# A hybrid decoder layer on one core: output weight sums made among the pairs, keys four tiles at a time, row sums of squares on ScalarE, and new orders at stage ends

## The chip, the core and the metric

The kernel runs on one core of one Trainium2 chip. The metric is the device time of one execution in microseconds (us); the median of three runs is compared. A core has a matrix engine, TensorE (PE, with its weight loads shown apart as PEld), a vector engine, VectorE (DVE), an activation engine, ScalarE (ACT), GpSimd (POOL), and SyncE (SP). Here SP issues most transfers from memory; POOL issues stores and accumulating loads.

## What is computed

One layer over 1024 tokens of width 1024, with 256 memory tokens, in float32:

```python
h = rms_norm(x, norm_g); z = h @ w_in                      # 11 blocks of 1024 columns
u = gelu(z_u); v = layer_norm(gelu(z_v))                   # branch A: chunked spatial gate
br_a = u * (tril(w_s) @ v + b_s) * silu(z_ga)              # in chunks of 128 tokens
glu = z_ba * sigmoid(z_bb)                                 # branch B
br_b = silu(layer_norm(causal_depthwise_conv(glu, 31 taps))) * silu(z_gb)
k, v = split(rms_norm(mem) @ w_kv)                         # branch C: 4 heads of 256
br_c = softmax(q k^T / 16) v * silu(z_gc)
merged = sum over n of sigmoid(z_mn) * (br_n @ w_branch[n])
out = rms_norm(x + merged @ w_out, final_norm_g)
```

## The kernel before

All products are made of float32 operands split in two halves, a rounded high half (ACT, `split`, line 74) and the rest as low half (DVE, line 75); three matmuls (high by high, high by low, low by high) stand for one. A matmul takes 128 x 128 weights and 256 or 512 columns. Engines run their instructions in order, each with its own queue. The order on a queue is not the one written: a planner lays out the instructions at build time by modelled costs, earlier written ones first among those that are ready, and hands out buffers as they come free. Loads marked `keep` stay in their written order on SP. Buffers: 39 slots of 1024 columns (`slot`), 6 for operands (`op`), 3 for raw weights, 4 each of `sum` and `half`.

Stages, in order of time:

- **Keys** (line 231). For each of 8 key tiles `e`, 8 steps of the contraction times 3 matmuls of 256 columns; the weights of one tile come as one transfer of 512 KB, and all of the memory (transposed, with its gain, `mhi` and `mlo`) is needed by the first tile. `mean_rsqrt` sums squares over partitions with one-column f32 matmuls (line 109); `spread` brings a row of factors to all partitions with f32 matmuls on diagonal matrices (lines 120, 121). `sumsq` makes squares on ACT and adds them on DVE.
- **Values** (line 280), 96 matmuls of 512 columns; then branch A's `v` by token (line 322), during which the sums of squares of x are finished, spread and used.
- **Pairs** (lines 364 to 414): 4 rounds of 10 blocks; each pair makes two column tiles of a block by a Strassen scheme with 7 products of 12 matmuls, accumulated in the banks x, y and z. `pend` carries the last two products into the next pair. `pump(n)` lets n steps of the depthwise convolution run on DVE between pairs; `spump` does the same for `wsum`, which loads quarters of branch B's output weights, adds them by accumulating loads on POOL, splits the sum and stores both halves for the later product.
- **Branch projections** A and C (line 656, `merge`), with attention in between. In C's, the convolution's channel mean and variance are made (`center`, `conv_rstd`) and `normed` finishes branch B's tiles `cm`.
- **Branch B's projection** and then **the output projection** (line 864, `oprod`): 7 products each, again by Strassen's scheme, on 2 x 2 blocks of 512. A product is 4 blocks of 12 matmuls, one for each 128 rows, accumulated in `px` or `py`; two blocks share one tile of two banks. Branch B's weight sums come from memory (`swload`); the output weights are loaded raw (`wraw`), subtracted (`sub`, line 957), and split (`wsplit`) on the spot.
- **End** (`yadd`): the residual is added, rows are squared and summed on ACT, scaled and stored.

Of the kernel before, what the change touches and what calls it, by code (L numbers as in the profile page):

```python
# [16 lines left out]
P = 128  # L17
# [22 lines left out]
def trunk(ctx, tc, xt, x, memt, wf, wv, wkf, wkv, wbr, wb1, wo, wst, bs, cols, fng, out):  # L40
# [66 lines left out]
    def mean_rsqrt(ssum, n, eps, ps):  # L107
        for i in range(n):
            T.matmul(ps[:, i:i + 1], ssum[:, i * P:(i + 1) * P], ones[:, 0:1], start=True, stop=True)
        a = small.tile([P, n], F32, tag=f"ms{n}", name=nm("ms"))  # L110
        V.tensor_scalar(a, ps[:, :n], 1.0 / D, eps, ALU.mult, ALU.add)
        return rsqrt(a, n)

    def spread(r, n, dst, mk):
        for i0 in range(0, n, 4):
            w = min(4, n - i0)
            ps = mk()
            for i in range(w):
                dg = small.tile([P, P], F32, tag="dg", name=nm("dg"), bufs=4)
                V.tensor_scalar(dg, ident, r[:, i0 + i:i0 + i + 1], None, ALU.mult)  # L120
                T.matmul(ps[:, i * P:(i + 1) * P], ones, dg, start=True, stop=True)
            A.copy(dst[:, i0 * P:(i0 + w) * P], ps[:, :w * P])

# [22 lines left out]
    onesd = const.tile([P, P], F32, name="onesd")  # L146
    G.memset(onesd, 1.0 / D)
# [9 lines left out]
    ahead = []  # L157

    def kv_ahead(n):
        i = len(ahead)  # L160
        while i < min(n, 2 * KT):
            t = slot(s="kvraw")
            keep(nc.sync.dma_start(out=t, in_=wkf[i] if i < KT else wkv[i - KT]))
            ahead.append(t)
            i += 1

    ahead.append(slot(s="kvraw"))
    mraw = [slot(shape=(P, 4, M), s="mraw") for _ in range(2)]
    keep(nc.sync.dma_start(out=ahead[0][:, :H], in_=wkf[0][:, :H]))
    keep(nc.sync.dma_start(out=mraw[0][:, :2, :], in_=memt[0][:, :2, :]))  # L170
    keep(nc.sync.dma_start(out=mraw[0][:, 2:, :], in_=memt[0][:, 2:, :]))
    keep(nc.sync.dma_start(out=ahead[0][:, H:], in_=wkf[0][:, H:]))
    keep(nc.sync.dma_start(out=mraw[1], in_=memt[1]))
    kv_ahead(2)
    xr = [None] * KT

    def x_load(k):
        xr[k] = slot(s="xr")
        keep(nc.sync.dma_start(out=xr[k], in_=xt[k]))

    mhi2 = [slot(F32R, (P, 4, M), "mhi") for _ in range(2)]
# [3 lines left out]
    for k in range(KT):  # L185
# [5 lines left out]
    xsum = slot(s="xsum")  # L191
    kv_ahead(3)
# [25 lines left out]
    for e in range(KT):  # L218
        kv_ahead(e + NAHEAD)
        x_load(e)  # L220
        if e:
            hi, lo = wchunk(None, ahead[e])
        else:
            hi, lo = op((P, 1024), "whi"), op((P, 1024), "wlo")
            for v in (slice(0, H), slice(H, 2 * H)):
                split(ahead[0][:, v], hi[:, v], lo[:, v])
        ps = bank()
        for k in range(KT):
            ks = slice(k * P, (k + 1) * P)
            for j, (w, m) in enumerate(((hi, mhi), (hi, mlo), (lo, mhi))):  # L230
                T.matmul(ps[:, :M], w[:, ks], m[k], start=(k == 0 and j == 0), stop=(k == KT - 1 and j == 2))  # L231
        late.append((e, ps))
        if e == 0:
            msum = slot(s="msum")[:, :M]
            for k in range(KT):
                sumsq(mraw[k // 4][:, k % 4, :], msum, k == 0, M)
        if e == E0:
            mr = mean_rsqrt(msum, MT, RMS_EPS, bank())
        if e == E1:
            spread(mr, MT, mrb, bank)  # L240
        if e >= E1:
            while late:
                k_out(*late.pop(0))
        if e >= XLAG:
            x_gain(e - XLAG)

# [11 lines left out]
    nsq = 0  # L258

    def squares(n):  # L260
        nonlocal nsq
        for k in range(nsq, min(nsq + n, KT)):
            sumsq(xr[k], xsum, k == 0, S)
            nsq = k + 1

    for hf in range(2):
        pst = [bank() for _ in range(MT)]
        for c in range(4):
            kv_ahead(KT + hf * 4 + c + NAHEAD)
            hi, lo = wchunk(None, ahead[KT + hf * 4 + c])  # L270
            i = hf * 4 + c
            if i < XLAG:
                x_gain(KT - XLAG + i)
# [8 lines left out]
            if i >= SQ0:  # L282
                squares(1)
# [25 lines left out]
    for th in range(2):  # L309
        va = [slot(s="va") for _ in range(4)]  # L310
        for ch in range(2):
            pst = [bank() for _ in range(4)]
            for c in range(4):
# [11 lines left out]
                if th == 0:  # L325
                    if i == 0:
                        squares(KT)
                        xrs = mean_rsqrt(xsum, TT, RMS_EPS, bank())
                        rb = slot(s="rb")
                        spread(xrs, TT, rb, bank)  # L330
                    else:
# [41 lines left out]
    def pair(blk, p, consume):  # L373
# [12 lines left out]
        o12 = operand(a12)  # L386
        V.tensor_tensor(s3, a11, a21, ALU.subtract)
        V.tensor_tensor(s4, a12, s2, ALU.subtract)
        prod(z, o12, B[1][0], True, True)
        ca, cb = slot(s="ca"), slot(s="cb")  # L390
# [718 lines left out]
```

## Time and profile before

| | |
|---|---|
| median of 3 runs | 1335.52 us (1333.23 to 1335.55) |
| profiled execution | 1335.1 us |
| its span, first to last instruction | 1333.2 us |
| PE busy | 1308.3 us (98%) |
| DVE busy | 1107.5 us (83%) |
| ACT busy | 612.8 us (46%) |
| mean granted clock of PE | 0.996 |
| moved by DMA | 219.84 MB, 165 GB/s over the span |

Rows of the profile name an instruction by its line in the kernel, engine, operation and the tiles that it writes and reads (out<-in). Matmuls are pipelined, and their ends are modelled, so a matmul's duration is longer than the distance to the next.

### The profile page before, as it was taken

The numbers are of one execution on the slowest core, as the hardware profiler recorded it, in microseconds if no ns is written. First come the engines' busy times: TensorE is split into PE (matmuls) and PEld (weight loads), VectorE is DVE, ScalarE is ACT, GpSimd is POOL, SyncE is SP. The second block draws the span as 40 slices with busy tenths as digits, with TensorE's granted clock in tenths as the row PEclk, the third lists the DMA queues.
The fourth block names the chain that finished last, engine by engine and source line by source line (L and its number), as shares of the span: only waits on it lengthen the run. The fifth ranks groups of instructions, "written<-read, shape, count | busy, mean of one in ns | idle before, by whom it ended". The sixth has DMA issues, their size and how long they took to land.

```text
span 1333.2 us, 16301 instructions
## 1 busy us (share of the span) xinstructions
PE 1308.3 (98%) x6036; PEld 1090.6 (82%) x6036; DVE 1107.5 (83%) x1506; ACT 612.8 (46%) x1005; POOL 88.8 (7%) x162
## 2 busy tenths in 40 slices
PE   8999999999999999999999999999999999999896
PEld 7888888888888888888888888887888888888785
DVE  6799769979977997986996996796797486975996
ACT  6757645434444444534444444345543352442345
POOL 0000000111100110100100000001000010000000
PEclk9999999999999999999999999999999999999999
DMA  9634444554634554454543214338554354657513
GB/s 375 245 109 160 141 144 146 170 166 145 195 128 141 172 174 153 173 135 157 154 150 125 95 48 127 123 114 302 180 182 174 114 218 157 240 213 283 211 32 127
DMA packets 72223, 219.84 MB, mean 165 GB/s; under 512 B 7248, under 2 KB 16592, under 8 KB 72144
## 3 DMA queue, kind: packets, MB, share of 16 engines
q1 hardware_dynamic: 50512, 140.79, 30.8%
q0 software_dynamic: 21344, 77.60, 17.3%
q8 instruction: 47, 0.77, 0.2%
q10 hardware_dynamic: 288, 0.42, 0.1%
q14 instruction: 32, 0.26, 0.1%
HBM read 156.92 MB, written 61.87 MB: 164 GB/s over the span
## 4 chain that ended last, share of the span: by engine, by line
PE 91%; DVE 5%; ACT 2%; issue 1%; DMA 0%; SPq 0%; DVEq 0%; ACTq 0%
PE x L365 33%; PE y L365 16%; PE acc L656 13%; PE z L365 8%; PE acc L864 7%; PE b L322 6%; PE b L231 2%; PE acc L694 2%; PE acc L730 2%; PE b L280 1%; PE sp L534 1%; DVE y L972 1%; DVE op L75 1%; DVE gate L957 1%; DMA mraw<-in_memt 0%
## 5 line engine op out<-in xcount | busy, mean ns | idle before, releaser
L365 PE MATMUL x<-T,op 128*128 128x512 f32 x1440 | 347.5, 390 | 0.7 <-ACT u L404 0.7
L365 PEld LDWEIGHTS x<-T,op 128*128 128x128 f32 x1440 | 269.9, 188 | 57.4 <-ACT u L404 1.1
L74 ACT CAST op<-sum 128x512 fp32r<-128x512 f32 x160 | 99.4, 622 | 131.2 <-PE z L365 50.7
L456 DVE SCALAR_TENSOR_TENSOR conv<-cb,col,conv 128x994 f32<-128x994 f32 (+14 forms) x120 | 151.9, 1266 | 0.5
L75 DVE TENSOR_TENSOR op<-sum,op 128x512 fp32r<-128x512 f32 x160 | 109.1, 686 | 25.6 <-ACT op L74 25.2
L365 PE MATMUL x<-B,op 128*128 128x512 f32 x480 | 115.5, 389 | 0.0
L365 PE MATMUL z<-B,op 128*128 128x512 f32 x480 | 115.3, 389 | 0.0
L365 PE MATMUL y<-T,op 128*128 128x512 f32 x480 | 115.3, 389 | 0.0
L365 PE MATMUL y<-B,op 128*128 128x512 f32 x480 | 115.3, 389 | 0.0
L456 DVE SCALAR_TENSOR_TENSOR conv<-ca,col,conv 128x994 f32<-128x994 f32 (+14 forms) x90 | 113.9, 1266 | 0.3
L74 ACT CAST op<-raw 128x512 fp32r<-128x512 f32 x120 | 74.3, 620 | 78.9 <-PE y L365 77.4
L75 DVE TENSOR_TENSOR op<-raw,op 128x512 fp32r<-128x512 f32 x120 | 82.0, 687 | 29.7 <-ACT op L74 29.5
L365 PEld LDWEIGHTS y<-B,op 128*128 128x128 f32 x480 | 90.1, 188 | 18.7
L365 PEld LDWEIGHTS y<-T,op 128*128 128x128 f32 x480 | 90.1, 188 | 18.7
L365 PEld LDWEIGHTS x<-B,op 128*128 128x128 f32 x480 | 90.1, 188 | 18.7
L365 PEld LDWEIGHTS z<-B,op 128*128 128x128 f32 x480 | 90.1, 188 | 18.7
L656 PE MATMUL acc<-bhi,whi 128*128 128x512 f32 x256 | 80.3, 395 | 0.9 <-DVE ca L414 0.9
L656 PE MATMUL acc<-bhi,wlo 128*128 128x512 f32 x256 | 79.7, 390 | 0.0
L656 PE MATMUL acc<-blo,whi 128*128 128x512 f32 x256 | 79.4, 391 | 0.0
L864 PE MATMUL acc<-q,sw 128*128 128x512 f32 x288 | 65.4, 389 | 0.0
L864 PEld LDWEIGHTS acc<-q,sw 128*128 128x128 f32 x288 | 54.1, 188 | 11.2
L404 ACT COPY u<-x 128x512 f32<-128x512 f32 x40 | 23.5, 588 | 80.6 <-PE x L365 80.6
(258 smaller groups left out, 2190.9 us busy)
## 6 DMA issues: line engine op xcount, KB each, us to landing
raw<-in_wf SPq DMA_DIRECT2D x80, 512.0 KB, 3.6
sw<-sw SPq DMA_DIRECT2D x28, 512.0 KB, 6.5
raw<-in_wv SPq DMA_DIRECT2D x16, 512.0 KB, 3.6
raw<-in_wbr SPq DMA_DIRECT2D x16, 512.0 KB, 5.9
gate<-g SPq DMA_DIRECT2D x16, 512.0 KB, 4.9
ws<-in_wb SPq DMA_DIRECT2D x14, 512.0 KB, 4.4
sw<-wsh POOLq DMA_DIRECT2D x14, 512.0 KB, 2.9
sw<-ws POOLq DMA_DIRECT2D x14, 512.0 KB, 3.2
```

What stands on the lines that cost most here:

```text
L74: A.copy(hi, src)
L75: V.tensor_tensor(lo, src, f(hi), ALU.subtract)
L231: T.matmul(ps[:, :M], w[:, ks], m[k], start=(k == 0 and j == 0), stop=(k == KT - 1 and j == 2))
L280: T.matmul(pst[m], a[k][:, ms], w[:, ws], start=(k == 0 and j == 0), stop=(k == KT - 1 and j == 2))
L322: T.matmul(pst[t], q[:, a, ts_], w[:, ws], start=(k == 0 and j == 0), stop=(k == KT - 1 and j == 2))
L365: T.matmul(ps, w[:, a, ks], m[k][:, b, :], start=(start and k == 0 and j == 0), stop=(stop and k == 3 and j == 2), skip_group_check=not start)
L404: A.copy(u3, x)
L456: V.scalar_tensor_tensor(out=a[:, PAD - j:], in0=g[:, :n], scalar=col[:, cw + j:cw + j + 1], in1=a[:, PAD - j:], op0=ALU.mult, op1=ALU.add)
L656: T.matmul(ps[:, hf, :], w[:, ks], m[k][:, hf * H:(hf + 1) * H], start=(k == 0 and j == 0), stop=(k == KT - 1 and j == 2))
L694: T.matmul(ps[:, i, :], q[a][:, d, i * P:(i + 1) * P], kk[:, b, d, :], start=(d == 0 and j == 0), stop=(d == 1 and j == 2))
L730: T.matmul(ps[:, d, :], vv[:, a, m, d * P:(d + 1) * P], p2[b][:, m, :], start=(m == 0 and j == 0), stop=(m == MT - 1 and j == 2))
L864: T.matmul(ps[t], a[k][i][:, ts_], w[k][n], start=(start and k == 0 and j == 0), stop=(k == 3 and j == 2), skip_group_check=not start)
```

## The change

- Keys: the packed key weights are cut so that one transfer holds two steps of the contraction for four tiles. Two groups of four tiles run 4 steps each, each step with 2/8 of the contraction for four accumulators. Ten f32 matmuls on a tile of ones are put first on PE.
- Sums of squares: the memory and x are loaded a second time by rows (tokens on partitions), and ACT's Square accumulates each row's sum. `spread` splits the factors in two halves and uses one 512-column matmul of each half for four diagonals.
- Convolution statistics: sum and sum of squares are split (`wchunk`) and averaged by `tokmean`, which leaves the result in all partitions; `conv_rstd` computes the root there, on 128 x 1024.
- Output weight sums: `wsum` handles the output weights too, so 28 sums instead of 14 are made among the pairs; stores of a sum are issued behind the first load of the next; `spump` makes three steps a pair instead of two. The output projection loads both halves.
- Orders: in the last pair the product into z comes after the copy of x; three tiles of branch A are split before that pair; the pump before it is shorter. The last block of the last product is computed in two halves of 256 columns. Row statistics of the output are accumulated half by half, and the final scaling is shared by DVE (640 columns) and ACT.

```diff
-    def spread(r, n, dst, mk):
+    def diagonals(r, n):
+        rh = small.tile([P, n], F32R, tag=f"rh{n}", name=nm("rh"))
+        rl = small.tile([P, n], F32R, tag=f"rl{n}", name=nm("rl"))
+        split(r, rh, rl)
+        groups = []
         for i0 in range(0, n, 4):
             w = min(4, n - i0)
+            dg = wpool.tile([P, 2, 4, P], F32R, tag="op", name=nm("dg"), bufs=NOP)
+            for j, v in enumerate((rh, rl)):
+                V.tensor_tensor(dg[:, j, :w, :], ident[:, None, :].broadcast_to([P, w, P]),
+                                f(v)[:, i0:i0 + w, None].broadcast_to([P, w, P]), ALU.mult)
+            groups.append((i0, w, dg))
+        return groups
+
+    def spread(groups, dst, mk):
+        for i0, w, dg in groups:
             ps = mk()
...
+            for j in range(2):
+                T.matmul(ps[:, :w * P], onesr, dg[:, j, :w, :].rearrange("p a b -> p (a b)"), start=(j == 0),
+                         stop=(j == 1))
             A.copy(dst[:, i0 * P:(i0 + w) * P], ps[:, :w * P])
+
+    def square(src, dst):
+        A.activation(out=src, in_=src, func=AF.Square, accum_out=dst)
...
+    kload(0, slice(0, H))
+    mload(0)
+    kload(0, slice(H, 2 * H))
+    for j in range(1, 4):
+        mload(j)
+        kload(j)
+    mtok = [slot(s="mtok") for _ in range(MT)]
+    kload(4)
+    for t in range(MT):
+        sload(mtok[t], mem[t * P:(t + 1) * P, :])
+    warm = bank("warm")
+    for _ in range(NWARM):
+        T.matmul(warm[:, :P], ones, ones, start=True, stop=True)
...
+            for kk2 in range(2):
+                k = 2 * j + kk2
+                for e in range(4):
+                    ks = slice(kk2 * H + e * P, kk2 * H + (e + 1) * P)
+                    for n, (w, m) in enumerate(((hi, mhi), (hi, mlo), (lo, mhi))):
+                        T.matmul(pst[e][:, :M], w[:, ks], m[k], start=(k == 0 and n == 0),
+                                 stop=(k == KT - 1 and n == 2))
...
+        if g == 0:
+            k3 = half("k3")
+            A.copy(k3[:, :M], pst[3][:, :M])
+            pst[3] = k3
...
     def squares(n):
+        for _ in range(n):
+            t = min(xtok)
+            square(xtok.pop(t), xss[:, t:t + 1])
+            if t + NRAW < TT:
+                xt_load(t + NRAW)
...
-    def pair(blk, p, consume):
+    def pair(blk, p, consume, last=False):
...
+        def second():
+            o12 = operand(a12)
+            prod(z, o12, B[1][0], True, True)
+            V.tensor_tensor(ca[:, :H], z, p1, ALU.add)
...
+        if not last:
+            second()
...
         u3 = half("u3")
         A.copy(u3, x)
+        if last:
+            second()
...
-    def wsum(i, j):
+    def wsum(w, i, j):
         t = slot(F32R, s="ws")
+        for n, b in enumerate((SUMB, SUMO)[w][i]):
+            src = (wb1, wo)[w][b + j]
             if n:
                 G.dma_start(out=f(t), in_=src, accum_op=ALU.add)
             else:
                 nc.sync.dma_start(out=f(t), in_=src)
+                flush()
             yield
         hi = slot(F32R, s="wsh")
         split(f(t), hi, t)
+        unstored.extend(((sdram[w, i, j][0], f(hi)), (sdram[w, i, j][1], f(t))))
         yield
...
+    csr = wchunk(None, csum)
+
+    def tokmean(v):
+        ps = acc()
+        for hf in range(2):
+            for j in range(2):
+                T.matmul(ps[:, hf, :], onesd, v[j][:, hf * H:(hf + 1) * H], start=(j == 0), stop=(j == 1))
+        return ps
...
     def conv_rstd():
         nonlocal crs
-        crs = mean_rsqrt(csq, TT, LN_EPS, misc())
+        ps = flat(tokmean(wchunk(None, csq)))
+        a, s, y = slot(s="ca"), slot(s="cs"), slot(s="crb")
+        for hf in range(2):
+            v = slice(hf * H, (hf + 1) * H)
+            V.tensor_scalar(a[:, v], ps[:, v], LN_EPS, None, ALU.add)
+            A.activation(out=s[:, v], in_=a[:, v], func=AF.Sqrt)
+            V.reciprocal(out=y[:, v], in_=s[:, v])
+            V.tensor_tensor(s[:, v], y[:, v], y[:, v], ALU.mult)
+            V.tensor_tensor(s[:, v], s[:, v], a[:, v], ALU.mult)
+            V.tensor_scalar(s[:, v], s[:, v], -0.5, 1.5, ALU.mult, ALU.add)
+            V.tensor_tensor(y[:, v], y[:, v], s[:, v], ALU.mult)
+        crs = y
...
-    o, w = [gop(v) for v in a11], wpair([wsplit(r) for r in t2])
+    oprod(py, o, w, True)
+    o, w = [gop(v) for v in a11], wn
+    wn = swload(1, "5", False)
...
+    oprod(py, o, w, False, 3)
+    for t in range(3):
+        ypart(t, 1, H, 2 * H, py[t], 2)
+        if t:
+            yend(t - 1)
+    ypart(3, 1, H, H + M, py[3][:, :M], 3)
+    yend(2)
+    ypart(3, 1, H + M, 2 * H, py[3][:, M:], 2, 1)
+    yend(3)
...
-SPUMP = 1
+SPUMP = 2
```

`ypart` adds the product to a row tile, squares it on ACT with an accumulated sum, multiplies it by the final gain and folds the sum into the row's mean; `yend` takes root and reciprocal, scales and stores the row tile.

## Rows read from the trace of the kernel before

**Rows 1.** The page, part 1: busy us (share) and instructions of each engine.

```profile
PE 1308.3 (98%) x6036; PEld 1090.6 (82%) x6036; DVE 1107.5 (83%) x1506; ACT 612.8 (46%) x1005; POOL 88.8 (7%) x162
```

**Rows 2.** Windows: span; busy of PE, PEld, DVE, ACT, POOL; clock, DMA share, GB/s.

```profile
16.00:35.30 19.30, 19.30 (x163) 19.30 (x163) 15.22 (x33) 11.79 (x20) 1.75 (x3) 1.00 1.03 409
161.60:921.00 759.40, 759.40 (x3415) 631.27 (x3416) 657.21 (x835) 326.74 (x519) 62.76 (x108) 1.00 0.46 148
541.30:560.30 19.00, 19.00 (x85) 15.76 (x84) 18.91 (x25) 8.94 (x14) 1.60 (x3) 1.00 0.44 150
1162.30:1237.00 74.70, 74.70 (x331) 61.86 (x331) 51.83 (x80) 22.29 (x38) 0.00 (x0) 1.00 0.69 258
1237.00:1275.00 38.00, 34.19 (x143) 27.24 (x142) 37.84 (x56) 14.64 (x27) 0.00 (x0) 0.96 0.42 155
```

**Rows 3.** Waits of PE: us in total, times, longest.

```profile
PE b L231 <- ACT mhi L187: 6.4, 2, 5.4
PE acc L864 <- DVE olo L75: 2.2, 1, 2.2
...
PE x L365 <- ACT u L404: 0.7, 1, 0.7
PE acc L121 <- DVE dg L120: 0.6, 1, 0.6
```

**Rows 4.** The chain of waits: start us, us, what.

```profile
9.61 10.51 PE b L231 x60
...
35.39 10.01 PE b L280 x44
...
1162.53 74.59 PE acc L864 x329
```

**Rows 5.** Timeline of ACT at the start: start us, us, instruction [idle before].

```profile
9.05 1.71 ACT L187 ACTIVATE mhi<-mraw,col 128x256 fp32r<-128x256 f32 x4 [1.00 <-DMA mraw<-in_memt]
10.66 2.01 ACT L74 CAST whi<-kvraw 128x1024 fp32r<-128x1024 f32 x2
12.57 0.41 ACT L126 ACTIVATE msum<-mraw 128x256 f32<-128x256 f32 x1
```

**Rows 6.** Groups of PE by form: busy us, mean ns | idle before.

```profile
L121 PE MATMUL b<-dg,ones 128*128 128x128 f32 x20 | 2.8, 280 | 0.0
...
L798 PE MATMUL acc<-csum,onesd 128*128 128x512 f32 x4 | 2.0, 592 | 0.0
L109 PE MATMUL b<-ones,xsum 128*128 128x1 f32 x16 | 1.8, 245 | 0.0
```

**Rows 7.** Groups of DVE by form, whole span: reciprocals.

```profile
L100 DVE RECIPROCAL rs_y<-rs_s 128x1 f32<-128x1 f32 x8 | 1.1, 163 | 2.9 <-ACT rs_s L99 2.8
...
L100 DVE RECIPROCAL rs_y<-rs_s 128x8 f32<-128x8 f32 x2 | 0.4, 199 | 0.3 <-ACT rs_s L99 0.3
```

**Rows 8.** Timeline of DVE between the convolution's statistic and branch B's product.

```profile
1121.60 0.17 DVE L111 TENSOR_SCALAR ms<-acc 128x8 f32<-128x8 f32 x1 [3.63 <-PE acc L109]
...
1131.64 4.87 DVE L786 SCALAR_TENSOR_TENSOR cm<-cm,col,crb 128x1024 f32<-128x1024 f32 x4 [0.16 <-ACT crb L122]
...
1155.44 1.89 DVE L75 TENSOR_TENSOR blo<-cm,bhi 128x512 fp32r<-128x512 f32 x3
```

**Rows 9.** Timeline of ACT in branch B's third product.

```profile
1189.76 1.07 ACT L879 COPY u<-acc 128x512 f32<-128x512 f32 x2 [4.71 <-PE acc L864]
```

**Rows 10.** The end: PE's last row, DVE's scaling (by form), last output transfer.

```profile
1321.12 0.39 PE L864 MATMUL acc<-olo,op 128*128 128x512 f32 x1
...
L986 DVE TENSOR_SCALAR y<-y,rs_y 128x512 f32<-128x512 f32 x1 | 0.5, 485 | 0.0
...
1329.22 0.35 ACTq L985 DMA_DIRECT2D out<-y  x1
```

**Rows 11.** All waits, one row; DVE's group by form of a weight sum's split.

```profile
ACT op L74 <- PE y L365: 118.7, 63, 2.1
...
L75 DVE TENSOR_TENSOR ws<-ws,wsh 128x1024 fp32r<-128x1024 f32 x14 | 17.1, 1220 | 0.6 <-ACT wsh L74 0.6
```

More of the change, by code (lines that the diff above doesn't have):

```diff
@@ L190, in trunk @@
     mrb = const.tile([P, M], F32, name="mrb")
-    xsum = slot(s="xsum")
-    kv_ahead(3)
+    mss = small.tile([P, MT], F32, tag="mss", name="mss", bufs=1)
+    xss = small.tile([P, TT], F32, tag="xss", name="xss", bufs=1)
     kdram = [spill("kd", F32, (P, 2, 2, M)) for _ in range(HEADS)]
@@ L216, in x_gain @@
                                op0=ALU.mult, op1=ALU.subtract)
[L218 to L245, printed above, removed]
+    vraw = [None] * KT
@@ L281, in trunk @@
                                  stop=(k == KT - 1 and j == 2))
-            if i >= SQ0:
+            if i < 2:
+                for _ in range(2):
+                    k_out(*late.pop(0))
+            if i == 1:
+                for t in range(NRAW):
+                    xt_load(t)
+            if i >= 3:
                 squares(1)
@@ L574, in spump, with branch_tile @@
                 sums.pop(0)
+                if not sums:
+                    flush()
+    bhi, blo = [None] * KT, [None] * KT
+    def branch_tile(e, val):
+        bhi[e] = slot(F32R, s="bhi")
+        blo[e] = slot(F32R, s="blo")
+        split(val, bhi[e], blo[e])
     bra = {}
@@ L596, in trunk @@
             spump(1)
-            pair(blk, p, kept(fn, then))
+            if (p, i) == (3, 9):
+                for e in range(NPRE):
+                    branch_tile(e, bra[e])
+            pair(blk, p, kept(fn, then), (p, i) == (3, 9))
             if i == 3:
@@ L795, in trunk @@
             cm = [load(cdram[e], s="cm", eng=G) for e in range(KT)]
-            ps = acc()
-            for hf in range(2):
-                T.matmul(ps[:, hf, :], onesd, csum[:, hf * H:(hf + 1) * H], start=True, stop=True)
-            A.copy(csum, flat(ps))
+            A.copy(csum, flat(tokmean(csr)))
             csq = slot(s="csq")
@@ L804, in trunk @@
         if d == 4:
-            crb = slot(s="crb")
-            spread(crs, TT, crb, misc)
+            crb = crs
             normed(0)
@@ new lines, in yend @@
+    def yend(i):
+        m, s, y, t, rr = fa[:, i, 1:2], *[fr[:, i, j:j + 1] for j in range(4)]
+        A.activation(out=s, in_=m, func=AF.Sqrt)
+        V.reciprocal(out=y, in_=s)
+        V.scalar_tensor_tensor(out=t, in0=y, scalar=m, in1=y, op0=ALU.mult, op1=ALU.mult)
+        V.tensor_scalar(t, t, -0.5, 1.5, ALU.mult, ALU.add)
+        V.tensor_tensor(rr, y, t, ALU.mult)
+        rows = slice(i * P, (i + 1) * P)
+        w = {3: 640, 2: 640, 1: 640}.get(i, 0)
+        v = ys[i]
+        if w:
+            V.tensor_scalar(v[:, :w], v[:, :w], rr, None, ALU.mult)
+            nc.sync.dma_start(out=out[rows, :w], in_=v[:, :w])
+        A.activation(out=v[:, w:], in_=v[:, w:], func=AF.Copy, scale=rr)
+        (A if i == 3 else nc.sync).dma_start(out=out[rows, w:], in_=v[:, w:])
```

293 lines of the change are left out of this document (142 added, 151 removed).

## The prediction, written before the result was known

> **What bounds the kernel now.** I began with the page's busy times [rows 1]: TensorE (PE) is busy for 1308.3 of 1333.2 us. So only three things can move the time: work that PE does, gaps of PE, and what stands before its first and behind its last matmul. The windows by stage say where the gaps are [rows 2]: the stage of 40 pairs (161.6 to 921) and the first product over blocks (1162.3 to 1237) have none, although VectorE (DVE) is full in single pairs; the stretch 1237 to 1275 has 3.8 us, with DVE busy for 37.84 of 38. The waits of PE name them one by one [rows 3]; before its first matmul PE waits 5.4 us. The chain of waits [rows 4] prices the start: the first 60 key matmuls after the second wait take 10.51 us, while at full pace 163 take 19.30, 0.12 each [rows 2]; the values begin at 35.39. A 512-column matmul takes 74.59/329 = 0.227 us. In the tail [rows 10] the last matmul ends near 1321.5 and the last output transfer is issued at 1329.22.
>
> The sum is made against the profiled execution, 1335.1 us (span 1333.2 and 1.9 around it); the median of the runs, 1335.52, is 0.03% above it. A measurement of this kernel can tell about 0.2%, 2.7 us, from no change.
>
> **1. Keys.** Today the first step needs all of the memory (1.5 MB with its weights) for its 24 matmuls; afterwards a step takes one eighth of the contraction through four key tiles. Transfers land in the order of issue. The fifth, 1.5 MB in, ends a wait at 9.05 [rows 5]; in the new order those 1.5 MB hold the weights of the first two steps and their memory. So at 9.05 the second step can be split: 1.0 for the high half (10.66: two casts in 2.01), 1.22 for the low one [rows 11]; as two matmuls go ahead of the low half, the step starts in effect at 11.1. The first step ends by 10.6 even at half the clock (24 x 0.21). The other seven are 7 x 24 x 0.12 = 20.2; each needs 0.79 MB, which the 409 GB/s of this stretch [rows 2] bring in 1.9 us, under the 2.9 of a step. With two new 256-column matmuls (0.24) the values start at 31.5 instead of 35.39: 3.9. The clock takes part of it: those 60 matmuls lost 10.51 - 7.2 = 3.3 us at the lower of its levels (1.2 for 2.4 GHz, by their pace). Ten warming matmuls are put into PE's idle first 5 us; if the pace rises as long after the first of them as it did before, at 16 after a start at 5.4, it is full from the second step on, less some half microsecond. I take 3.4; if it stays low until 16, 23 matmuls cost 0.09 more, 2.1, and 1.6 is left. ScalarE (ACT) gets a copy of the fourth accumulator between the halves, which waits for PE, and the next step's cast is written behind it. But the order written is not the order run: casts of the next steps ran at 10.66, before squares written ahead of them [rows 5]. If it did hold, cast and low half would cost 2.2.
>
> **2. Statistics of x.** The sums by one-column and 128-column f32 matmuls go: 16 records of line 109 and 16 of line 121 [rows 6] are 1.8 + 16 x 0.14 = 4.0 us busy, 0.85 of it real, since modelled ends overlap the next start: 3.4. Four 512-column ones replace them, 0.9. Gain 2.5. ACT squares as many elements as before, now over the 22 us of value matmuls (96 x 0.227) and beside them. DVE's adds of squares go. The 4.2 MB of x by rows and the 1 MB of memory by rows are new on SP's queue, ahead of the next weights, which at 409 GB/s land some 2 us before they are needed; without that cover one transfer of 0.5 MB costs 1.3.
>
> **3. End of the pairs.** The last pair does another product between two that share a bank: the wait of 0.7 on ACT's copy [rows 3] goes. Nothing else of that hand-over changes.
>
> **4. Convolution statistics.** Channel sums: four f32 records, 2.0 busy [rows 6], become four at 0.227: 0.85 x 2.0 - 0.9 = 0.8 gained. Squares: 16 one-column records become four: 0.6. The spread over partitions goes whole, 16 x 0.14 x 0.85 = 1.9, and the wait of 0.6 [rows 3]: 2.5. Together 3.9, of which 3.1 come behind the statistic. In exchange DVE computes the root over 1024 columns, not 8. The trace has no reciprocal wider than 8 columns: 163 ns for 1, 199 for 8 [rows 7]. The low end is a plain 512-column pass, 0.63 [rows 8]. The slope between the two, 5.1 ns a column, gives 2.8 us; if half of the eight columns hide in the fixed start, it is 9 ns and 4.6 us, the high end. I take 2.8, the plain slope of the same operation. Today DVE has the statistic at 1121.60 and the first normalised tile starts at 1131.64 [rows 8]. Afterwards it has it at 1120.8, the first reciprocal starts at 1122.1 (a scale, a root), then two reciprocals 5.6, eight other passes over 512 columns 4.6 (0.485 [rows 10] to 0.63), three 1024-column passes of the merge in between 3.4: 1135.7, which is 4.1 later. What is late next: the low halves for the first sum's product, written last, at 1155.44 to 1157.3 [rows 8]. PE, 3.1 earlier than the 1162.53 of [rows 4] or just before it, wants the second to fourth at about 1160.2 to 1161.6. The lead is 4.1 and the delay 4.1: no wait, and nothing to spare. Gain 3.9.
> A rule stands against this: the Trainium skill, "VectorE: DVE Perf Modes", First, the fixed hardware budget, says that a reciprocal iterates its divide with a repeat count of 8. By that page it would be 8 cycles a column at 0.96 GHz, an estimate of 4.3 us for 512 columns and of 1320.6 for the sum; the slope that the trace shows is 4.9 cycles, and no row here is wide enough to tell.
>
> **5. Output weight sums.** At the end, 8 subtractions and 14 splits of 1024 columns go from DVE and ACT; their halves come by 28 transfers. The 3.8 us of waits between 1237 and 1275 [rows 2] are for DVE (olo, 2.2 [rows 3], is such a split). Ahead of the third product it loses six of the subtractions and two splits, 9.8 us by 1.22, and is done about 2 us before PE asks. The granted clock fell there too, to 0.96 in the mean: 0.04 x 38 = 1.5, part of it inside the waits, 0.9 on top. Gain 4.7. The transfers: 4 x 0.52 MB in a product of 10.9 us (48 x 0.227) is 192 GB/s, with x about 250; the first product moved 258 with no wait [rows 2].
> The sums move into the pairs: 14 more splits (1.22 on DVE, 1.0 on ACT), 14 loads on SP, 14 accumulating loads and 28 stores on POOL; one split a pair in 28 pairs where there was one in two. I cost them at nothing: ACT waits 118.7 us in 63 places for PE to free an operand's buffer [rows 11], so operands stand ready several products ahead, and DVE has 102 us free in the stage. A sum's load may wait for a slot on SP while loads of weights are queued behind it; these have the same lead.
>
> **6. Tail.** Row statistics are accumulated by halves, small steps fused, and DVE takes 640 columns of the scaling. The last block is cut in two (24 x 0.12 for 12 x 0.227, 0.16 lost) so that its first half can be read early. That it can, I doubt: ACT's two copies of a pair start together at 1189.76 after 4.71 idle [rows 9], when the second block is done, 2.7 after the first; what shares a tile is read when all of it is written. So behind the last matmul: adds from +0.25; ACT's squares (0.41 for 256 columns [rows 5], some 0.6 for 512), each with a read of the accumulator, end at +3.1; a scale, a root and four small steps at 0.2 (0.163 for one [rows 7]) to +4.5; 640 columns (0.485 x 640/512) to +5.1; issue at +5.2, where it is +7.7 today. Gain 2.5 - 0.16 = 2.3; 3.8 if the half can be read early, 0.8 if the work of the row before it stands in front.
>
> **Sum.** 3.4 + 2.5 + 0.7 + 3.9 + 4.7 + 2.3 = 17.5; 1335.1 - 17.5 = 1317.6.
>
> **Rivals.**
> A, slower: the weight sums cost the pairs. For it: DVE is busy for 18.91 of 19.0 us in a pair such as 541.3 to 560.3 [rows 2], and POOL and the slots carry twice the sums. Against: the buffers ahead of PE. Uncovered, 14 casts and subtractions are 31 us: 1349. Slower than before from 1.4 us of PE's time per added split. 0.05.
> B, wide reciprocals at the high end, 4.6 us: the delay is 7.7 against a lead of 4.1, PE waits 3.6 for the low halves of the first sum's product: 1321.2. For it, eight columns are few to read a slope from, and the lead has nothing to spare; against, the slope as it stands. 0.2. The rule of the Trainium skill named in part 4 would bring the same mechanism.
> C, the start: the clock stays low until 16, or the copy between the halves holds back the casts, 1.8 to 2.2 less; one late transfer of x on top: 1319.4 to 1321. 0.15.
> D, the weights of the second product come late: one microsecond for each of its seven products behind the first: 1324.6. For it, slots come back only when a product ends; against, two products' sums fit ahead. 0.1.
> E, start at its best (3.9) and an early read of the last half (3.8): 1315.6. 0.1.
> F, some edits do nothing (DVE still holds the third product, the tail stays): 7.0 less, 1324.6. 0.05.
> The forecast as it stands has 0.35.
>
> **How the numbers follow.** The likeliest is 1317.6. E and a microsecond of overlapping small waits go down to 1313; B and C together up to 1325, D and F to 1324.6. I leave out A and what lies beyond those ends: 1312 to 1325. Faster by over 0.2% is all but A and a pile-up of C, D and F: 0.93; within, 0.03; slower, 0.04.
>
> **What would show it.** Keys: values begin at 31 to 32 us. x: no one-column records. Roots: how long a 512-column reciprocal takes, and whether PE waits for a low half at the first sum's product. Pairs: PE busy all of that stage. Third product: no wait, clock 1.00. Tail: 5.2 us from the last matmul to the last issue. The prediction falls if PE shows gaps inside the pairs, or if loads end its waits in the second product.

## The result, and the profile after

The changed kernel takes 1349.85 us (median of 4 runs, 1345.98 to 1355.2) against 1334.38 (4 runs, 1332.86 to 1335.55): ratio 1.0120, 95% interval 1.0103 to 1.0137. It is slower by 15.5 us, where 17.5 us faster was forecast and 1312 to 1325 was the range. The profiled run is the slowest of the four, 1355.2 us with a span of 1353.5.

Windows cut at the same places of the work show where the time went: start of the keys, of the values, of branch A's `v`, a fixed product inside the pairs (the first one of `bsb`, line 573 after, 506 before), the first merge, branch B's first product, the last matmul. The kernel before (span; busy PE, PEld, DVE, ACT, POOL; clock, DMA share, GB/s):

```profile
0.00:5.40 5.40, 0.00 (x1) 0.00 (x1) 0.70 (x2) 2.46 (x4) 0.98 (x8) 1.00 0.63 207
5.40:35.20 29.80, 28.83 (x200) 28.04 (x201) 23.22 (x47) 20.40 (x38) 1.75 (x3) 1.00 1.02 407
35.20:57.60 22.40, 22.34 (x99) 17.94 (x98) 17.06 (x24) 15.47 (x24) 1.59 (x3) 1.00 0.66 260
57.60:212.00 154.40, 153.98 (x694) 127.16 (x693) 125.19 (x205) 95.77 (x139) 7.86 (x15) 1.00 0.41 138
212.00:929.30 717.30, 715.75 (x3222) 594.51 (x3220) 628.52 (x795) 307.61 (x488) 61.57 (x105) 1.00 0.46 149
929.30:1162.40 233.10, 232.43 (x1157) 196.32 (x1158) 177.66 (x189) 102.80 (x193) 15.05 (x28) 1.00 0.52 182
1162.40:1321.50 159.10, 154.99 (x673) 126.66 (x671) 130.32 (x226) 62.74 (x113) 0.00 (x0) 0.99 0.46 171
1321.50:1333.20 11.70, 0.01 (x1) 0.00 (x0) 4.87 (x24) 5.58 (x10) 0.00 (x0) 0.73 0.59 237
```

The changed kernel, same columns:

```profile
0.00:12.10 12.10, 4.14 (x20) 3.96 (x20) 3.01 (x4) 5.55 (x9) 0.84 (x7) 0.83 0.85 293
12.10:39.20 27.10, 26.28 (x194) 25.79 (x195) 17.86 (x35) 18.82 (x32) 0.68 (x1) 0.89 1.03 410
39.20:65.90 26.70, 22.55 (x99) 17.71 (x97) 17.06 (x30) 22.39 (x42) 3.15 (x6) 1.00 0.85 342
65.90:218.50 152.60, 152.56 (x664) 125.83 (x665) 119.92 (x194) 91.01 (x133) 11.02 (x21) 0.99 0.50 164
218.50:951.40 732.90, 719.57 (x3222) 595.15 (x3221) 641.31 (x809) 315.22 (x501) 86.44 (x142) 1.00 0.57 181
951.40:1190.00 238.60, 231.03 (x1129) 194.62 (x1130) 188.36 (x187) 103.68 (x193) 15.05 (x28) 0.99 0.51 179
1190.00:1343.70 153.70, 152.91 (x685) 126.61 (x683) 109.16 (x206) 51.04 (x101) 0.00 (x0) 1.00 0.61 236
1343.70:1353.50 9.80, 0.00 (x0) 0.00 (x0) 5.10 (x19) 3.20 (x11) 0.00 (x0) 0.62 0.56 214
```

Row by row: the values start 4.0 later (39.2 for 35.2); they take 26.7 for 22.4, +4.3; the stage of `v` up to the fixed place -1.8; the pairs +15.6; the merges +5.5; the two output stages -5.4; the end -1.9. The sum is 20.3, which is 1353.5 - 1333.2. The profile is that of the slowest run: it lies 5 us above the median, and which stage those 5 belong to isn't shown. PE is busy for about as long as before (1308.3 and 1309.1 us in the two sums, the second with 4.1 of warming), so nearly all of it is idle time. PE's waits, which answer to [rows 3]:

```profile
PE x L425 <- ACT u L462: 8.8, 5, 5.4
PE acc L732 <- DVE wlo L75: 7.5, 1, 7.5
PE b L269 <- ACT mhi L210: 6.9, 1, 6.9
PE b L380 <- ACT whi L74: 2.9, 1, 2.9
PE x L425 <- DVE op L75: 2.6, 1, 2.6
...
PE acc L732 <- DVE ca L481: 0.9, 1, 0.9
...
PE acc L938 <- DVE op L75: 0.8, 1, 0.8
```

The wait for the memory's high halves (`mhi`) was there before, with its start, and so were that for `ca` and, with 0.3, the last one, for `op` in the output projection; the others are new. Gone are the waits for `olo` and for `u` at the pairs' end. Behind the two longest of them inside the work PE ran at the lower of its two levels, 1.2 for 2.4 GHz, before it was back at 1.00:

```profile
349.10:352.70 3.60, 3.60 (x9) 2.83 (x10) 3.60 (x5) 0.98 (x2) 0.31 (x1) 0.50 0.54 218
1177.93:1182.10 4.17, 4.17 (x10) 3.34 (x11) 4.17 (x5) 0.72 (x1) 0.00 (x0) 0.50 1.02 415
```

Nine and ten matmuls of 512 columns in these stretches, at 0.227 us when the clock is full, are 1.6 and 1.9 us more than the waits themselves. With the waits of 12.4 us in the pairs (8.8, 2.6 and 1.0 for `z`) that accounts for 14.0 of the 15.6.

**The start.** The timeline of ACT and the first key matmul:

```profile
8.37 1.04 ACT L74 CAST whi<-kvraw 128x1024 fp32r<-128x1024 f32 x1 [2.04 <-DMA kvraw<-in_wkf]
...
10.62 1.04 ACT L74 CAST whi<-kvraw 128x1024 fp32r<-128x1024 f32 x1 [1.21 <-DMA kvraw<-in_wkf]
...
11.57 1.70 ACT L210 ACTIVATE mhi<-mraw,col 128x256 fp32r<-128x256 f32 x4
...
12.13 0.80 PE L269 MATMUL b<-mhi,whi 128*128 128x256 f32 x2 [6.92 <-ACT mhi L210]
```

The memory's first high halves run at 11.57, although a quarter of the memory is now enough for the first step; before the change the last four of the eight began at 9.05 [rows 5]. In ACT's queue they stand behind the casts of the second and third weights, and both casts waited for their transfers (2.04 and 1.21 us idle). The warming matmuls had ended at about 5; after 7 us of idling PE ran the first keys at a granted clock of 0.50, the level of 1.2 GHz (23 matmuls in the 5.9 us after 12.1, 45 in the next 6.0).

**The pairs.** The longest wait, with what led to it:

```profile
330.22 0.42 SPq L629 DMA_DIRECT2D ws<-in_wb  x1
...
336.59 0.88 POOL L627 DMA_DIRECT2D ws<-in_wb  x1 [11.94 <-DMA ws<-in_wb]
...
344.57 1.04 ACT L74 CAST wsh<-ws 128x1024 fp32r<-128x1024 f32 x1 [8.32 <-DMA ws<-in_wb]
...
348.47 0.57 ACT L462 COPY u<-x 128x512 f32<-128x512 f32 x1
...
349.09 3.35 PE L425 MATMUL x<-T,op 128*128 128x512 f32 x7 [5.39 <-ACT u L462]
```

A sum's first load is issued at 330.22, the accumulating one at 336.59 when the first has landed; it lands 8 us later. The cast of the sum, at 344.57, ends 8.32 us of idling of ACT. The copy of x that PE waits for stands behind it and comes at 348.47. ACT's waits over the whole run, two rows:

```profile
ACT wsh L74 <- DMA ws<-in_wb: 23.9, 6, 8.3
...
ACT wsh L74 <- DMA ws<-in_wo: 21.4, 6, 5.4
```

Before the change no such wait exists. I took the start of each cast of a sum less the issue of its last transfer (timelines of both kernels): a median of 23 us before, with 3 of 14 casts under 9 us; 6.6 us after, with 19 of 28 under 9. The accumulating transfers take 6.1 to 6.2 us in the median to land (transfers by line), where they took 5.6 before.

**The convolution.** The wide reciprocals, in the groups by form of DVE (busy us, mean ns | idle before):

```profile
L870 DVE RECIPROCAL crb<-cs 128x512 f32<-128x512 f32 x2 | 6.6, 3324 | 0.4 <-ACT cs L869 0.4
```

And the timeline around the last merge:

```profile
1147.33 1.05 ACT L74 CAST whi<-raw 128x1024 fp32r<-128x1024 f32 x1 [1.73 <-PE acc L732]
...
1174.27 2.47 DVE L882 SCALAR_TENSOR_TENSOR cm<-cm,col,crb 128x1024 f32<-128x1024 f32 x2
...
1176.66 1.21 DVE L75 TENSOR_TENSOR wlo<-raw,whi 128x1024 fp32r<-128x1024 f32 x1
...
1177.93 1.22 PE L732 MATMUL acc<-bhi,wlo 128*128 128x512 f32 x2 [7.52 <-DVE wlo L75]
```

A 512-column reciprocal takes 3.32 us. The high half of the last weight is cast at 1147.33; its low half, at 1176.66, stands in DVE's queue behind merges and normalised tiles; DVE is busy without a break from 1145 to 1178.

**The end.** The adds on the last blocks and the last output transfer, which answers to [rows 10]:

```profile
1343.71 1.35 DVE L1053 TENSOR_TENSOR y<-y,acc 128x512 f32<-128x512 f32 x3 [0.76 <-PE acc L938]
...
1349.24 0.36 ACTq L1079 DMA_DIRECT2D out<-y  x1
```

The last matmul ends at 1343.7; the transfer is issued 5.6 us behind it, where it was 7.7.

### The profile page after: what moved, and what is told of

Same layout as the page of the kernel before. It is cut to its first block, busy times and chain, and to the rows that moved or that the text cites. A ratio compares the mean times of both kernels' runs of the same rounds, so it can differ in the third digit from the quotient of the medians.

```text
span 1353.5 us, 16391 instructions
## 1 busy us (share of the span) xinstructions
PE 1309.0 (97%) x6006; PEld 1089.7 (81%) x6006; DVE 1101.8 (81%) x1479; ACT 610.9 (45%) x1017; POOL 117.2 (9%) x203
## 4 chain that ended last, share of the span: by engine, by line
PE 78%; DVE 10%; DMA 7%; issue 3%; ACT 2%; SPq 0%; POOL 0%; DVEq 0%; POOLq 0%; ACTq 0%
PE x L425 24%; PE y L425 12%; PE acc L938 11%; PE acc L732 11%; PE b L380 7%; PE z L425 6%; DMA ws<-in_wb 2%; DVE conv L523 2%; PE acc L770 2%; DVE op L75 2%; PE acc L806 2%; DMA ws<-in_wo 2%; DMA raw<-in_wf 1%; PE b L269 1%; PE b L332 1%
## 5 line engine op out<-in xcount | busy, mean ns | idle before, releaser
L938 PEld LDWEIGHTS acc<-q,sw 128*128 128x128 f32 x288 | 54.1, 188 | 11.2
L732 PEld LDWEIGHTS acc<-bhi,wlo 128*128 128x128 f32 x256 | 48.5, 190 | 18.0 <-DVE wlo L75 7.9
```

The source lines that it names most:

```text
L732: T.matmul(ps[:, hf, :], w[:, ks], m[k][:, hf * H:(hf + 1) * H], start=(k == 0 and j == 0), stop=(k == KT - 1 and j == 2))
L938: T.matmul(ps[t][:, v], a[k][i][:, ts_], w[k][n][:, v], start=(start and k == 0 and j == 0), stop=(k == 3 and j == 2), skip_group_check=no ...
```

## The experiments

Each kernel is the changed one with the edit shown, unless it says otherwise, and ran beside the kernel before, whose medians were 1334.4 to 1335.2.

### 1. Splits one pair later

```diff
 def wsum(w, i, j):
     ...
-    hi = slot(F32R, s="wsh")
-    split(f(t), hi, t)
-    unstored.extend(...)
+    unsplit.append((npair[0], w, i, j, t))   # split and stored one pair later
     yield
```

> Changed kernel, with each of the 28 splits of weight sums written one pair (about 19 us) later; loads, stores and their number stay. Theory (a cast at the head of ScalarE's queue waits for its accumulating transfer, and the pair's copies stand behind it): ScalarE's waits for the sums' transfers, 45 us in 12 places, go; TensorE's waits inside the pairs fall from about 14 us to under 3; the time falls from 1350 to 1336-1339. Rival (the added splits themselves fill ScalarE and VectorE): the waits stay above 10 us and the time within 3 us of 1350. Second rival (slots: a sum holds its slots one pair longer): waits for casts turn into waits for loads of weights, time 1345-1350.

1338.67 us (7 runs), ratio 1.0033 (1.0019 to 1.0047): 11.2 us regained. ACT's waits for the sums' transfers are gone and no wait inside the pairs reaches 0.5 us; from the fixed place to the first merge it is 717.0 us, against 717.3 before the change. The shortest time from the issue of a sum's last transfer to its cast is now 13 us, the median 37. So 28 splits, 56 loads and 56 stores cost the pairs nothing when no cast stands and waits. The longest of PE's waits that are left:

```profile
PE acc L743 <- DVE wlo L75: 7.5, 1, 7.5
```

### 2. The root over 8 columns

```diff
 def conv_rstd():
-    ps = flat(tokmean(wchunk(None, csq)))
-    ...                                       # root on 128 x 1024
+    crs = mean_rsqrt8(csq, TT, LN_EPS, misc())   # 16 one-column records, root on 128 x 8
 ...
-    crb = crs
+    spread8(crs, TT, crb, misc)                  # 16 records of 128 columns
```

> Changed kernel, with the convolution's reciprocal root computed as before the change: 16 records of one-column sums, a root over 8 columns, and 16 records of 128 columns to spread it. Theory (two reciprocals of 3.3 us and eight passes over 512 columns fill VectorE, so that the low half of a weight comes 7.5 us late in the third merge): that wait goes, TensorE pays about 2.5 us for the small matmuls, net 4.5-5.5 us faster than the changed kernel, 1344.5-1345.5. Rival (the low half was merely put behind other work in VectorE's order): at least 3 us of the wait stays, and the time is within 2 us of 1350.

1345.83 us, ratio 1.0083 (1.0067 to 1.0100): 4.0 us less than the changed kernel. The 7.5 us wait is gone; the merges take 231.5 us, 7.1 less than in the changed kernel and 1.5 less than before it. Why the median shows 4.0 and not 7 isn't shown; the likely place is the pairs, whose waits vary: in one profile each they are 12.4 us in the changed kernel and 8.5, 3.3 and 8.4 in experiments 2 to 4, which have the same splits, and the four runs of the changed kernel lie 9.2 us apart. Single edits can therefore be read to the microsecond only by stage.

### 3. Squares of x from the transposed tiles

```diff
-    square(xtok.pop(t), xss[:, t:t + 1])      # x by rows, 4.2 MB more to load
+    sumsq(xr[k], xsum, k == 0, S)             # as before the change
 ...
-    xrs = mean_rsqrt(xss, TT, RMS_EPS)
+    xrs = mean_rsqrt8(xsum, TT, RMS_EPS, bank())
```

> Changed kernel, with the sums of squares of x as before the change: from the transposed tiles, without the 4.2 MB of x by rows on the load queue; eight one-column sums come back, about 0.9 us of TensorE. Theory (loads bound the start of the changed kernel, 410 GB/s without a break from 10 to 60 us): the third stage (value tokens by wv) starts 4-5 us earlier than its 65.9, its waits for casts of weights (4 us) go; net 2.5-4 us faster, 1346-1347.5. Rival (ScalarE's squares hold up the casts, not the loads): there are as many squares as before, so the start stays at 65-66 and the time within 1 us of 1350 or slower.

1347.57 us, ratio 1.0098 (1.0083 to 1.0113): 2.3 less. The stage of `v` starts at 61.9 instead of 65.9, as the theory of the loads has it. But the edit has a price of its own in that stage: 2.6 us of waiting for the diagonals, since the one-column sums and the spread now stand directly behind each other, 1.9 for the sums and one more for the squares. The fixed place is reached at 221.4, later than the changed kernel's 218.5. So the 2.3 us in the median aren't the start's; they are within what the pairs' waits vary by.

### 4. The start in the order of landing

```diff
 def split(src, hi, lo):
-    A.copy(hi, src)
-    V.tensor_tensor(lo, src, f(hi), ALU.subtract)
+    keep(A.copy(hi, src), pin[0])              # kept in the order written
+    keep(V.tensor_tensor(lo, src, f(hi), ALU.subtract), pin[0])
 # the same in mem_gain and in the squares of the memory; pin[0] is on in the first four key steps
```

> Changed kernel, with ScalarE's and VectorE's work for the first four key steps pinned in the order in which its inputs land (cast of a weight, then the memory's halves of the same step, then the next cast). Theory (two costs in a row: the memory's high half stood behind two casts that wait for transfers; and loads bound the end of the values anyway): the first key matmul starts at 7-8 us instead of 12.1 and the values at 35-36 instead of 39.2, but the third stage starts no more than 1.5 us earlier than 65.9; net 0-1.5 us. Rival (the order alone is the cost of the start): the third stage starts 4 us earlier, net 4 us, 1346.

1350.10 us (1347.65 to 1350.8), ratio 1.0112 (1.0097 to 1.0127): no gain in the time. The first key matmul starts at 5.6 and the values at 33.9, 5.3 us earlier; the stage of `v` at 62.4, 3.5 earlier, nearer to the rival's 4 than to the theory's 1.5. The fixed place is reached 3.5 earlier too; the medians don't show it, for which the pairs are again the likely place. That loads do take part of it back shows in the wait for the stage's first cast, 2.9 in the changed kernel:

```profile
PE b L387 <- ACT whi L76: 4.6, 1, 4.6
```

The longest wait that is left inside the keys isn't for weights to land (ACT's timeline and PE's wait):

```profile
18.25 1.28 ACT L102 ACT_TABLE_LOAD   x1
...
20.87 1.04 ACT L76 CAST whi<-kvraw 128x1024 fp32r<-128x1024 f32 x1
...
PE b L274 <- ACT whi L76: 1.8, 1, 1.8
```

By 20 us PE has started 96 key matmuls, four whole steps; the fifth step's weights have landed at 14.5. Their cast stands in ACT's queue behind the statistic of the memory by rows, which landed at 15.8 and 17.1: two squares, a table load for the root and the root, from 15.8 to 20.9.

### 5. The four edits together

The diffs of experiments 1 to 4 in one kernel.

> Changed kernel with all four edits of the runs before: splits a pair later, root over 8 columns, squares of x from the transposed tiles, start in order of landing. Theory (four separate costs, two of which, the order of the start and the loads of x by rows, only give their time back together): first key matmul near 5.6 us, values from 34, third stage from 57; waits inside the pairs under 3; no wait in the third merges; output stage 5.5 us and tail 1.8 us shorter than before the change as in the changed kernel. Time 1324-1328, 7-11 us under the kernel before. Rival (the effects merely add, 11.2 + 4.0 + 2.3 + 0): 1331-1333. Rival (one mended wait opens another behind it): above 1333.

1328.51 us (1328.01 to 1329.34), ratio 0.9951 (0.9938 to 0.9963): 21.3 us under the changed kernel, where the four single runs give 17.2. With the waits in the pairs gone the start can be read: the stage of `v` starts at 56.5, 9.4 earlier than in the changed kernel, where order and loads alone gave 3.5 and 4.0. From there to the fixed place it takes 158.2 us, 3.8 more than before the change, 2.6 of it the wait of experiment 3, and the granted clock was 0.50 from 64.3 to 71.1, where it was 1.00 before; so the fixed place is reached at 214.7, against 217.6 in experiment 1 and 212.0 before the change. The windows of both stages:

```profile
33.40:56.50 23.10, 22.68 (x98) 17.83 (x98) 21.34 (x30) 19.42 (x30) 2.65 (x5) 1.00 0.79 318
56.50:214.70 158.20, 155.31 (x681) 127.52 (x681) 122.21 (x197) 93.58 (x138) 10.27 (x18) 0.98 0.44 147
```

In PE's waits it is the largest:

```profile
PE b L138 <- DVE dg L129: 2.6, 1, 2.6
```

### 6. The wide root with the last weights split early

To the kernel of experiment 5:

```diff
-    crs = mean_rsqrt8(...)                     # and spread8
+    ...                                        # the wide root of the change
     if d == 4:
+        for n in (5, 6, 7):
+            ready[2, n] = weights(2, n)        # ahead of the normalised tiles
```

> As the kernel with four edits, but with the wide root of the change and the weights of the last three third-branch merges split before the normalised tiles instead of behind them. Theory (VectorE is short of time by the two reciprocals; whatever stands last in its queue is late): the 7.5 us wait for the weight's low half goes, but the low halves of the first sum's operands come late instead, 2-5 us of wait at the first output product; TensorE saves 2.5 us of small matmuls; 0-3 us slower than the kernel with four edits. Rival (only the queue order cost time): no wait, 1-3 us faster than the kernel with four edits.

1331.09 us, ratio 0.9970 (0.9958 to 0.9982): 2.6 slower than experiment 5. The wait for the low half is gone and the merges take 228.8 us instead of 231.6, but the output stages 158.6 instead of 153.7. Of that, two waits in branch B's first product are 2.8, not for a low half but for loads of the sums' weights:

```profile
PE acc L967 <- DMA sw<-sw: 2.8, 2, 2.1
```

So the delay moves on, as the first theory has it, though to another place than it named. The trace shows the way: a product with a gate on DVE and the first issue of the sums' weights, in experiment 5 and then here:

```profile
1130.76 1.22 DVE L905 TENSOR_TENSOR gate<-gate,gate 128x1024 f32<-128x1024 f32 x1
...
1141.80 0.92 SPq L928 DMA_DIRECT2D sw<-sw  x2
...
1138.99 1.22 DVE L916 TENSOR_TENSOR gate<-gate,gate 128x1024 f32<-128x1024 f32 x1
...
1151.78 1.41 SPq L940 DMA_DIRECT2D sw<-sw  x3
```

With the wide root in front of it (1126.0 to 1136.7) DVE makes that product 8.2 us later; it frees the buffer that a gate's load waits for at the head of SP's queue, and the sums' weights, issued behind that load and the next, come 10.0 us later. Of the other 2 us some 1.5 are the clock, 0.50 from 1165.5 to 1168.9, behind the waits. No further run tests this.

### 7. The memory by rows later

To the kernel of experiment 5: its 1 MB is loaded behind the last key weight, its squares two steps later (the spread of its factors and the key outputs move back with them).

```diff
-    if i == 3:                                 # squares of mtok
+    if i == 5:
 ...
+    if i == 2:
+        for t in range(MT):
+            sload(mtok[t], mem[t * P:(t + 1) * P, :])
```

> As the kernel with four edits, but the memory by rows (1 MB) is loaded behind the last key weights instead of among them, and its squares stand behind the casts of the fifth and sixth key step. Theory (with the order mended, the key steps wait for their weights, 410 GB/s, and 1 MB is 2.5 us): values start 1.5-2.5 us earlier (32 instead of 34) and the time is 1-2.5 us lower. Rival (loads bound the end of the values in any order): values start earlier but the third stage does not; within 0.7 us.

A miss: 1334.46 us, ratio 0.9994 (0.9986 to 1.0003), 6 us slower than experiment 5. The squares of the memory now wait for their transfer at the head of ACT's queue, and a key weight's cast stands behind them, the order that cost 1.8 us in experiment 4; values start at 37.8.

```profile
22.36 1.06 ACT L154 ACTIVATE mtok<-mtok 128x1024 f32<-128x1024 f32 x1 [4.23 <-DMA mtok<-in_mem]
...
27.99 1.99 ACT L76 CAST whi<-kvraw 128x1024 fp32r<-128x1024 f32 x2
```

### 8. Without the warming matmuls

To the kernel of experiment 5:

```diff
-NWARM = 10
+NWARM = 0
```

> As the kernel with four edits, without the ten warming matmuls ahead of the first key. Theory (the warming lets the keys run at full rate from their first matmul at 5.6; without it the granted clock is 0.5 for the first 10 us of keys): key matmuls until about 15 us take 0.21 instead of 0.12 us, values start 1-2 us later, time 0.5-2 us higher. Rival (the loads are the bound of the key steps): values start at the same time, no difference.

1328.55 us, ratio 0.9950 (0.9936 to 0.9963): no difference. With warming PE starts 14 key matmuls up to 8 us, but then 11 and 6 in the next two stretches of 2 us, since operands are missing; without it 11, 10 and 10. By 12 us that is 31 in both, and from there both start 17 in 2 us and the values at 33.4 and 33.3. Without warming the matmuls are 0.21 us apart, the lower level, only until 9.5, and 0.12 from there on, not for the first 10 us as expected. What those 4 us cost is hidden by the operands: the casts of weights wait for their transfers, at 354 to 424 GB/s between 8 and 12.

### 9. Start and statistics as before the change

The kernel of experiment 5 with keys, values, and the sums of squares of memory and x, up to the pairs, replaced by those of the kernel before.

```diff
-    for g in range(2):                         # two groups of four key tiles
-        ...
+    for e in range(KT):                        # one key tile after the other
+        kv_ahead(e + NAHEAD)
+        x_load(e)
+        ...
```

> The kernel with four edits, but keys, values and the statistics of the memory and of x wholly as before the change (their order of loads too). What is left of the change: output weight sums early (splits a pair later), the last pair's order, the channel sums on split operands, the tail. Theory (the new start loses even in landing order, because its key steps wait for weights and its spread of x waits 2.6 us for the diagonals: a fixed place in the pairs' stage is reached at 214.7 against 212.0 before the change): 2-3 us faster than the kernel with four edits, 1325.5-1326.5. Rival (the new start is worth what the old one is): within 0.7 us of 1328.5.

1324.32 us, ratio 0.9922 (0.9910 to 0.9935): the fastest kernel of this study, 10.1 us under the kernel before. The fixed place is reached at 211.2 instead of 214.7. Its largest wait inside the pairs is 0.8. The parts of the change that it keeps were forecast at 0.7 + 0.8 + 4.7 + 2.3 = 8.5; some 0.9 of the 10.1 may be the buffer named in experiment 10.

### 10. The output sums alone

The kernel before with `wsum` for both weights (splits a pair later) and the output products on loaded sums; nothing else of the change.

```diff
-    o, w = [gop(v) for v in a11], wpair([wsplit(r) for r in t2])
+    o, w = [gop(v) for v in a11], wn
+    wn = swload(1, "5", False)
```

> The kernel before with one part of the change alone: the output weights' sums made among the pairs, each split a pair later, and the output products on loaded sums. The prediction's term for this is 4.7 us. Theory (the output stage of the changed kernel is 5.5 us shorter than before, and sums placed a pair later cost the pairs under 0.5): 1329-1330. Rival (the doubled sums cost the pairs even when no cast waits for a transfer): above 1331. The difference to the kernel with the start as before is then what the tail, the channel sums and the last pair are worth: 3-3.5 us.

1327.61 us, ratio 0.9944 (0.9930 to 0.9957): 6.8 us faster than the kernel before, more than either theory gave. In its profile the output stages take 153.6 instead of 159.1 us, 5.5; the rest is 0.7 at the fixed place, where the full clock came 1.4 us earlier, and 0.9 in the merges, where only the buffer of the spread's diagonals differs, less 0.6 in the pairs. Buffer and clock are no part of the sums, so their own share is 5.5 - 0.6 = 4.9, close to the 4.7 forecast. The waits for `olo` and for casts in the third product are gone:

```profile
PE acc L879 <- DVE op L77: 0.8, 1, 0.8
PE x L372 <- ACT u L416: 0.7, 1, 0.7
```

Between experiments 9 and 10 lie 3.3 us in the medians. In the profiles 2.0 of them are the tail (9.5 for 11.5 us behind the last matmul) and 0.6 the merges (the channel sums on split operands); the wait at the pairs' end, the row above, is there only in experiment 10.

## Why the prediction was wrong

**Sums among the pairs (part 5): the step that failed most.** "I cost them at nothing" rested on the operands that stand ready and on DVE's free time. Both held: experiment 1 has the same sums at no cost. What was not looked at is what the casts of the sums themselves wait for. They stand in ACT's own queue, and ACT runs its queue in order; with three steps a pair a sum's last transfer is issued under 9 us ahead of its cast in 19 of 28 cases, about as long as it takes to land. I had looked for a late load on SP, where weights are queued behind it, and not on the engine that uses it. Rival A named place, sign and even the time (1349), but by throughput, 31 us of casts uncovered, and experiment 1 shows that throughput costs nothing. It had 0.05. The gain at the output itself was 5.4 for 4.7 forecast, and experiment 10 shows it alone; one reading behind it was inexact, since 1.3 of the 3.8 us between 1237 and 1275 were a wait for a cast on ACT, and a wait of 0.8 is left there where none was forecast. The prediction's own sign of being wrong, gaps inside the pairs, is what came.

**Keys (part 1): -3.4 forecast, +4.0 measured.** The failing step is "the order written is not the order run", used there as comfort. It cuts both ways: the same planner put two casts that wait for transfers ahead of the memory's halves. With the order pinned the values start at 33.9 (experiment 4) against 31.5 forecast. Up to 20 us the keys keep the sum's pace (96 matmuls started for 98); 1.8 of the 2.4 us go where the fifth step's cast stands behind the memory's statistic on ACT, which the sum left out. The warming works and brings nothing (experiment 8), since operands are missing between 8 and 12, where a step's 0.79 MB was thought to come in time. Nor does the lower level always last until 16: with the old start the matmuls are 0.12 us apart from 16.1 on in the kernel before, from 14.7 in experiment 10 and from 9.5 in experiment 9. Rival C had a late start only from the clock and the copy. Two slips change nothing in the sum: a step takes a quarter of the contraction, not an eighth (its 24 matmuls are right), and 3.9 less 2.1 is 1.8, not 1.6.

**Statistics of x (part 2): -2.5 forecast.** The small matmuls brought 1.8 (the stage of `v`), with the clock at 0.50 from 66.0 to 69.4; in experiment 1, where it stayed at 1.00 there, the stage takes 151.3 us, 3.1 less than before. The factor 0.85 in their sums stands on no row. "Land some 2 us before they are needed" failed. The sum for it was in the trace of before: up to 57.6 its transfers leave the engines idle for 0.34 of 22.4 us, 7.6 us (windows above); 5.2 MB at 409 GB/s are 12.7, 5 us more than fit. The values took 4.3 longer. Experiment 3 takes 4.2 MB away and the stage of `v` starts 4.0 earlier; with the order mended, the same edit is worth 5.9 there (62.4 in experiment 4, 56.5 in experiment 5).

**Convolution (part 4): -3.9 forecast, +5.5 measured.** The reciprocal takes 3.32 us for 2.8, inside the range given: a term mis-sized by 0.5, twice. The trace doesn't agree with the estimate of 4.3 us by the Trainium skill, "VectorE: DVE Perf Modes", First, the fixed hardware budget, either: it is 1 us too long. The step that failed is "what is late next": not the low halves for the first sum's product but the last merge's weight, which the planner had put behind the normalised tiles, with 7.5 us of wait for rival B's 3.6. The wait, 1.9 of lower clock behind it and the 3.9 forecast for the small matmuls give the 5.5 measured, so that gain came. "No wait, and nothing to spare" should have been read as a warning: DVE has some 12 us of new work in this stretch (two reciprocals, 6.6, and ten passes over 512 columns of 0.4 to 0.7), and whatever stands last pays. Experiment 2 removes it, experiment 6 moves it on to SP's queue.

**End of pairs (part 3)**: right, the wait for ACT's copy is gone. The stage as a whole doesn't show its 0.7: it takes 718.3 us in experiment 9, which has the new order and a wait of 0.8 elsewhere, and 717.9 in experiment 10, which has neither. **Tail (part 6)**: right, 5.6 us for 5.2 forecast; -1.9 for -2.3. The halves of the last block are not read early, as doubted: the three adds at 1343.71 start behind the last matmul.

## What to carry to other kernels

An engine with an in-order queue is stopped by one instruction that waits for a transfer: ahead of any change that adds work fed by transfers, measure for each such instruction how long its transfer is issued before it, and keep that well above the time to landing. At the start it was the same, with the memory's halves behind casts that waited; the last merge's low half stood behind work that was merely long. Price a wait at more than its length: PE ran at the lower clock behind the longest ones. In a stage that loads as fast as it can, price every added byte at the stage's rate against the idle time of the transfers in the whole stage, not against one step. Where the sum gives a lead equal to the delay, forecast a wait, and ask what else stands in that engine's queue.

## What was not expected of the hardware

A reciprocal of 512 columns took 3296 to 3353 ns, 6.2 ns for each column behind the first, where the slope between 1 and 8 columns gave 5.1 [rows 7]. In the changed kernel an accumulating load of 512 KB took 6.1 to 6.2 us to land in the median, and 8.0 ahead of the longest wait, while the sums' plain loads took 4.5 to 5.2 and those of the pairs' weights 3.7.
